# A decoder layer on one core: the recurrent gate stage and the compression MLP's first layer in a new order

## The chip, the cores and the metric

The kernel runs on one core of a Trainium2 chip. The metric is device time in microseconds (us). Before the change it is 1894.97 us, the median of three runs (1893.92 to 1895.76).

The engines are named as the profile names them: PE is TensorE (matmuls), DVE is VectorE, ACT is ScalarE, POOL is GpSimd, SP is SyncE, which issues most of the transfers.

## The reference, cut to what matters

One layer is computed for 512 tokens and 1024 features: a gated linear recurrence and a sparse attention side by side, then an expert layer, then a gated embedding. The change touches the recurrence (`rg_lru`, after a causal convolution of width 4) and the MLP that compresses keys and values.

```python
xa = causal_dwconv(z_rx, conv_w[i], conv_b[i])
ha = rg_lru(xa, lru_wr[i], lru_br[i], lru_wi[i], lru_bi[i], lru_lam[i])
...
def rg_lru(x, w_r, b_r, w_i, b_i, lam):
    xb = xf.reshape(B, S, RNN_BLOCKS, RNN_BLOCK)
    r = sigmoid(einsum('bsnc,ncd->bsnd', xb, w_r) + b_r)
    ig = sigmoid(einsum('bsnc,ncd->bsnd', xb, w_i) + b_i)
    log_a = -LRU_C * r * softplus(-lam)
    a = exp(log_a)
    u = sqrt(-expm1(2.0 * log_a)) * (ig * xf)
    # h[t] = a[t] * h[t-1] + u[t], along the 512 tokens
...
def compress_blocks(t, idx, pe, w1, b1, w2, b2):   # once for keys, once for values
    blk = t[:, idx] + pe[:, None, :]
    hid = gelu(einsum('bgnf,fh->bgnh', flat, w1) + b1)   # f = 32 * 128, h = 256
    return einsum('bgnh,hd->bgnd', hid, w2) + b2
```

## The kernel before, in words

Features lie on the 128 partitions and tokens along the free dimension. A projection of 1024 to 128 features is a *chunk*: 24 matmuls over 8 blocks k of the input. Every fp32 matrix is held as a rounded high half and a low half (the rest), and each product is three matmuls, high by high, high by low, low by high (`mm3`, L131 to L134; in the profile these three lines stand for nearly every matmul). The high half is a cast (`L126` on ACT, `L128` on DVE), the low half a subtraction (`L129`). Nothing reorders the work: each engine runs its instructions in the order in which the code is written, so the order of Python calls is the schedule.

The stages around the change, in the order in which PE runs them:

1. **Eight `rx` chunks (L398) and two `kc` chunks (L472).** After the matmuls of chunk c its evacuation `ev_rx` (L373) runs: ACT writes `xa` with the last convolution tap (L380), DVE adds the other three taps (L382), ACT and DVE make the two halves of `xa` (`xhl`), DVE and POOL the halves of the gate weights (`lwhl`). The two gate products (`lru`, six matmuls) of chunk c follow the matmuls of chunk c+1 on PE; then ACT takes two sigmoids (L394), and DVE multiplies the input gate by `xa` (L395, the *gate product*). Behind each chunk one piece of a list `side` is issued, small DVE and ACT work. Before each chunk, `look` splits the weights of the chunk two ahead: DVE casts, POOL subtracts (in this stage).
2. **Ten chunks `rg` and `vc` (L550 to L564)**, in the order rg 0 to 5, vc 0, vc 1, rg 6, rg 7 (all are called `z_rg` in the trace). Between the k blocks of a chunk stand the steps of `compress` (L479): the MLP's *first layer*, 16 steps for the keys and 16 for the values, four matmuls each (`hid`, L491). A step at block k of chunk n is called where the table `CSTEP[n]` holds k. Each step needs one piece of `w1` (128 x 512 fp32). POOL issues its load (L449) into one of four buffers, ACT casts its high half (L455), DVE subtracts its low half (L464), PE uses both; the low half frees the buffer for the piece four further on. `LAW` is 3: step n casts the high half of piece n+2 and makes the low half of piece n+1.
3. In the same chunks `SIDE[n]` deals out the recurrence, again by block k: `lru_b` (L403: tanh and two exponentials on ACT, one multiplication on DVE), two square roots of four blocks each (L415), `lru_c` (L418: one multiplication, L420, and one scan, L421, on DVE), and the rotary sine and cosine.
4. **Two `v` stages (L574)**: values of the selected and of the window branch. The last seven first-layer steps stand in the first. Then come the recurrent output `hg`, the `ks`, `kw` and `w_a` chunks, `q`, and the attention.

Of the 16 steps of the values three stand in rg 6 (its first entry in `CSTEP` is the transposition that ends the keys, `hidT`, L498), six in rg 7 and seven in the first `v` stage. They need `blk` (L436 and the two lines of its halves), which DVE makes from vc 0 and vc 1. Pieces are counted through both: the values' first step is 16.

Of the kernel before, what the change touches and what calls it, by code (L numbers as in the profile page):

```python
# [17 lines left out]
OP = mybir.AluOpType  # L18
# [76 lines left out]
def tile_hybrid(ctx, tc, a, out, dbg=None):  # L95
    nc = tc.nc
    V, A, T, G, SP = nc.vector, nc.scalar, nc.tensor, nc.gpsimd, nc.sync
# [17 lines left out]
    def bank(name, tag="ax"):  # L115
        if tag == "ax":
            tag = "aaax"[turn[0] % 4]
            turn[0] += 1
        return ps.tile([128, 512], F32, name=name, tag=tag, bufs=NBK[tag])

    def f(ap):
        return ap.bitcast(F32)

    def split(hi, lo, src, eng=None, heng=None):
        if heng is None:
            A.copy(hi, src)  # L126
        else:
            heng.tensor_copy(hi, src)  # L128
        (eng or V).tensor_tensor(lo, src, f(hi), op=OP.subtract)  # L129

    def mm3(o, sh, sl, mh, ml, start, stop):  # L131
        T.matmul(o, sh, mh, start=start, stop=False)  # L132
        T.matmul(o, sh, ml, start=False, stop=False)  # L133
        T.matmul(o, sl, mh, start=False, stop=stop)  # L134
# [45 lines left out]
    side = []  # L180

    def run_side(n):
        for _ in range(n):
            if side:
                side.pop(0)()

    def look(keys):
        for key in keys:
            if key not in ready:
                w8_split(key[0], key)  # L190
# [4 lines left out]
    def run_post():  # L195
        while post:
            post.pop(0)()

    def gemm(jobs, nside=1, nxt=()):

        keys = [j[:2] for j in jobs] + list(nxt)
        for n, (name, i, mh, ml, evac) in enumerate(jobs):
            look(keys[n:n + 3])
            w = ready.pop((name, i))
            o = bank("z_" + name)
            if key0 == keys[n]:
                for q, (ws, m) in enumerate(((0, mh), (1, mh), (0, ml))):
                    for k in range(KD):
                        T.matmul(o, w[:, ws, k], m[:, k], start=q == 0 and k == 0, stop=q == 2 and k == KD - 1)
            else:  # L210
                for k in range(KD):
                    mm3(o, w[:, 0, k], w[:, 1, k], mh[:, k], ml[:, k], k == 0, k == KD - 1)
            run_post()
            r = evac(i, o)
            if r is not None:
                post.append(r)
            run_side(nside[n] if isinstance(nside, tuple) else nside)
# [4 lines left out]
    nhi = keep.tile([128, KD, S], F32R, name="nhi", tag="nx")  # L222
    nlo = keep.tile([128, KD, S], F32R, name="nlo", tag="nx")
    rms = const.tile([128, 4, NT], F32, name="rms")

    def t2(nm, sh=(128, S), dt=F32):
        return p.tile(list(sh), dt, name=nm, tag="t2", bufs=4)
# [131 lines left out]
    gx = at.tile([128, 8, S], F32, name="gx", tag="big0")  # L359
# [6 lines left out]
    def load_lru(c):  # L366
        w = p.tile([128, 2, 128], F32, name="lruw", tag="lruw")
        SP.dma_start(w, a["lru_w"][c])
        lru_load.append(w)

    load_lru(0)

    def ev_rx(c, o):  # L373
        def col(b):
            return par[:, b + c:b + c + 1]

        def cw(j):
            return par[:, P_CW + c * 4 + j:P_CW + c * 4 + j + 1]
        xa = t2("xa")
        A.activation(xa, o, AF.Identity, bias=col(P_CB), scale=cw(3))  # L380
        for s in range(1, 4):
            V.scalar_tensor_tensor(xa[:, s:], o[:, :S - s], cw(3 - s), xa[:, s:], op0=OP.mult, op1=OP.add)  # L382
        w = lru_load.pop()
        if c < 7:
            load_lru(c + 1)
        xh, wh = xhl[:, c % 4], lwhl[:, c]
        split(wh[:, 0], wh[:, 1], w, G, V)
        split(xh[:, 0], xh[:, 1], xa)

        def gates():  # L390
            for j in range(2):
                o2 = bank("lru", "t")
                mm3(o2, wh[:, 0, j], wh[:, 1, j], xh[:, 0], xh[:, 1], True, True)
                A.activation(gx[:, c] if j else rr[:, c], o2, AF.Sigmoid, bias=col(P_BI if j else P_BR))  # L394
            V.tensor_tensor(gx[:, c], gx[:, c], xa, op=OP.mult)  # L395
        return gates

    gemm([("rx", i, nhi, nlo, ev_rx) for i in range(8)], nxt=[("kc", 0), ("kc", 1)])  # L398

    a2s = {}  # L400

# [27 lines left out]
    def ev_kv(j):  # L429
        def ev(c, o):  # L430
            if c == 0:
                blk[j] = at.tile([128, 2, 16, 2, NG, NB], F32R, name="blk", tag="sm2")
            for ab in range(2):
                pe = par[:, P_PE + 32 * j + 16 * ab:P_PE + 32 * j + 16 * ab + 16]
                t = t2("blkt", (128, 16, NB))
                V.tensor_tensor(t, o.rearrange("p (n l) -> p l n", l=16)[:, :, ab:ab + NB],  # L436
                                pe[:, :, None].to_broadcast([128, 16, NB]), op=OP.add)
                split(blk[j][:, ab, :, 0, c], blk[j][:, ab, :, 1, c], t, V, V)
        return ev
# [4 lines left out]
    w1n = [0, 0, 0]  # L444

    def w1_load(upto):
        while w1n[0] < min(upto, 32):
            j, l0 = divmod(w1n[0], 16)
            G.dma_start(w1buf[w1n[0] % 4], a["cmp_w1"][j][:, 2 * l0:2 * l0 + 2].rearrange("p l c -> p (l c)"))  # L449
            w1n[0] += 1  # L450
# [10 lines left out]
    def w1_lo(upto):  # L461
        while w1n[2] < upto:
            n = w1n[2]
            V.tensor_tensor(w1hl[:, n % 4, 1], w1buf[n % 4], f(w1hl[:, n % 4, 0]), op=OP.subtract)  # L464
            w1n[2] += 1
            w1_load(n + 5)
# [2 lines left out]
    V.tensor_tensor(sel, ident[:, 0:62], ident[:, 62:124], op=OP.add)  # L469
    w1_load(4)  # L470
    lo_eng[0] = V
    gemm([("kc", i, nhi, nlo, ev_kv(0)) for i in range(2)], nside=(2, 1), nxt=[("rg", 0), ("rg", 1)])  # L472

    kcT = at.tile([128, 2, NB], F32, name="kcT")
    vchi = at.tile([128, 2, 128], F32R, name="vchi")
# [69 lines left out]
    hls = [None, None]  # L545
    w1_split(1)
    seq = [("rg", i) for i in range(6)] + [("vc", 0), ("vc", 1)] + [("rg", i) for i in range(6, 8)]
    CSTEP = [(), (), (1, 3, 5, 7), (1, 3, 5, 7), (1, 3, 5, 7), (0, 2, 3, 5, 7), (), (), (4, 5, 6, 7), (0, 1, 3, 4, 6, 7)]
    SIDE = [(5,), (), (), (0, 0), (0, 0), (1,), (0, 0, 4), (0, 3, 6), (1, 2, 5), (1, 4, 6)]
    for n, key in enumerate(seq):  # L550
        look(seq[n:n + 3])
        w = ready.pop(key)
        o = bank("z_rg")
        for k in range(KD):
            mm3(o, w[:, 0, k], w[:, 1, k], nhi[:, k], nlo[:, k], k == 0, k == KD - 1)
            if k in CSTEP[n]:
                next(comp, None)
            run_side(SIDE[n].count(k))
            if n == 9 and k == 3:
                hls[0] = pair("vs")  # L560
                for j in range(2):
                    pair_split("vs", None, j, hls[0])
        (ev_rg if key[0] == "rg" else ev_kv(1))(key[1], o)
# [12 lines left out]
    for br, n in enumerate(("vs", "vw")):  # L576
        hl = hls[br]
        os = [bank("v") for _ in range(NT)]
        for i in range(NT):
            ts = slice(i * 128, (i + 1) * 128)  # L580
            for k in range(KD):
                T.matmul(os[i][:, :256], nhi[:, k, ts], hl[0][:, k], start=k == 0, stop=False)
                T.matmul(os[i][:, :256], nlo[:, k, ts], hl[0][:, k], start=False, stop=False)
                if br == 0 and k % 4 == 3:
                    next(comp, None)
        if br == 0:
            for _ in comp:
                pass
            hghi = at.tile([128, 8, S], F32R, name="hghi", tag="big0")
            hglo = at.tile([128, 8, S], F32R, name="hglo", tag="big1")  # L590
            hg += [hghi, hglo]
            side += [lru_d(c) for c in range(8)]
            split(wgh, wgl, wg)
            hls[1] = pair("vw")
            for j in range(2):
                pair_split("vw", None, j, hls[1])
        else:
            look([("ks", 0), ("ks", 1)])
        for i in range(NT):
            ts = slice(i * 128, (i + 1) * 128)  # L600
            for k in range(KD):
                T.matmul(os[i][:, :256], nhi[:, k, ts], hl[1][:, k], start=False, stop=k == KD - 1)
            split(vhi[:, i, br], vlo[:, i, br], os[i][:, :256])
            run_side(1)
    run_side(len(side))
    dump("kcT", kcT)
    dump("hg", f(hghi))
# [42 lines left out]
    def ev_q(c, o):  # L650
# [4 lines left out]
        def score():  # L655
# [9 lines left out]
         nxt=[("w_a", 0), ("w_a", 1)])  # L665
# [175 lines left out]
    for n in range(1, len(blocks) + 1):  # L841
# [5 lines left out]
        if n < len(blocks):  # L847
# [4 lines left out]
            i, hp = blocks[n]  # L852
# [38 lines left out]
    for q in range(4):  # L891
# [31 lines left out]
        for i in range(NT):  # L923
            if q < 3:
                wo_lo(i)
            if nhl and i == 0:
                for j in range(2):
                    c = slice(j * 128, (j + 1) * 128)
# [579 lines left out]
    for hf in range(2):  # L1508
        c = slice(hf * 512, (hf + 1) * 512)
# [82 lines left out]
```

## Time and profile before

| what | value |
|---|---|
| median of three runs | 1894.97 us |
| the profiled execution's own time | 1896.81 us |
| its span, first to last instruction | 1895.0 us |
| PE busy | 1819.3 us, 96% of the span |
| DVE busy | 1401.5 us, 74% |
| ACT busy | 840.3 us, 44% |
| POOL busy | 648.8 us, 34% |
| granted PE clock, mean of the run | 0.988 |
| the stages the change touches | from 30 us to some 190 us of the span |

The profile comes from one execution, whose own time is 1.84 us above the median of the timed runs; 1.81 us of its time lie outside the span. A busy share is an average: what an edit in one stage is worth is read from that stage's waits. In a timeline row the first number is the start in us from the span's start, the second the length; brackets at the end name idle time of the engine before the row and what ended it. Ends of matmuls are modelled, so the distance between the starts of two PE rows is a safer measure than their lengths.

### The profile page before, as it was taken

The numbers are of one execution on the slowest core, as the hardware profiler recorded it, in microseconds if no ns is written. First come the engines' busy times: TensorE is split into PE (matmuls) and PEld (weight loads), VectorE is DVE, ScalarE is ACT, GpSimd is POOL, SyncE is SP. The second block draws the span as 40 slices with busy tenths as digits, with TensorE's granted clock in tenths as the row PEclk, the third lists the DMA queues.
The fourth block names the chain that finished last, engine by engine and source line by source line (L and its number), as shares of the span: only waits on it lengthen the run. The fifth ranks groups of instructions, "written<-read, shape, count | busy, mean of one in ns | idle before, by whom it ended". The sixth has DMA issues, their size and how long they took to land.

```text
span 1895.0 us, 26509 instructions
## 1 busy us (share of the span) xinstructions
PE 1819.3 (96%) x9817; PEld 1594.3 (84%) x9817; DVE 1401.5 (74%) x2658; ACT 840.3 (44%) x1274; POOL 648.8 (34%) x419
## 2 busy tenths in 40 slices
PE   7998999999999989999999999999999999999997
PEld 6777888777789879899999888888888899999986
DVE  6867607565633378999999967888888788888864
ACT  4464333344522434574674763333333333333443
POOL 3311454322135325335335321222222255556400
PEclk9999999899999999999999999999999999999999
DMA  4353232211015426697787998999999899999941
GB/s 171 105 183 97 89 101 67 67 56 45 23 67 178 190 87 202 233 365 257 275 331 258 335 357 298 355 358 352 347 355 353 304 338 324 348 337 350 363 178 45
DMA packets 179810, 433.29 MB, mean 229 GB/s; under 512 B 14560, under 2 KB 88032, under 8 KB 179680
## 3 DMA queue, kind: packets, MB, share of 16 engines
q1 hardware_dynamic: 119664, 241.96, 36.8%
q0 software_dynamic: 40288, 145.77, 21.5%
q10 hardware_dynamic: 19728, 43.86, 6.1%
q8 instruction: 77, 1.26, 0.3%
q14 instruction: 53, 0.43, 0.1%
HBM read 382.25 MB, written 49.28 MB: 228 GB/s over the span
## 4 chain that ended last, share of the span: by engine, by line
PE 73%; DVE 16%; ACT 4%; issue 4%; DMA 3%; POOL 0%; SPq 0%; DVEq 0%; ACTq 0%; POOLq 0%
PE va L132 9%; PE va L134 9%; PE va L133 9%; PE xu L134 7%; PE xu L132 7%; PE xu L133 7%; DVE ul L1087 2%; DVE oh L1259 2%; DVE gr L1288 1%; PE G L1236 1%; PE z_m L132 1%; PE z_m L133 1%; PE z_m L134 1%; DVE acc L1294 1%; PE sc L996 1%
## 5 line engine op out<-in xcount | busy, mean ns | idle before, releaser
L132 PE MATMUL xu<-x2hi,uh 128*128 128x384 f32 x1008 | 345.2, 342 | 4.7 <-ACT ac L1097 4.7
L134 PE MATMUL xu<-x2hi,ul 128*128 128x384 f32 x1008 | 340.6, 338 | 5.8 <-DVE ul L1087 5.8
L133 PE MATMUL xu<-x2lo,uh 128*128 128x384 f32 x1008 | 339.9, 337 | 0.0
L132 PE MATMUL va<-v,A 128*128 128x512 f32 x768 | 299.0, 389 | 1.5 <-ACT A L126 1.5
L134 PE MATMUL va<-v,A 128*128 128x512 f32 x768 | 298.8, 389 | 0.0
L133 PE MATMUL va<-v,A 128*128 128x512 f32 x768 | 298.8, 389 | 0.0
L1273 POOL DMA_INDIRECT gr<-in_peer_u,eidx x128 | 170.7, 1333 | 327.8 <-DVE gr L1288 250.5
L1273 POOL DMA_INDIRECT gr<-in_peer_v,eidx x128 | 187.8, 1467 | 267.5 <-DVE acc L1294 210.2
L126 ACT CAST v<-vring 128x1024 fp32r<-128x1024 f32 x128 | 134.7, 1052 | 262.7 <-issue 144.2
L129 DVE TENSOR_TENSOR v<-vring,v 128x1024 fp32r<-128x1024 f32 x128 | 156.5, 1223 | 67.8 <-ACT v L126 67.2
L132 PEld LDWEIGHTS xu<-x2hi,uh 128*128 128x128 f32 x1008 | 191.4, 190 | 7.0 <-ACT ac L1097 5.3
L134 PEld LDWEIGHTS xu<-x2hi,ul 128*128 128x128 f32 x1008 | 191.1, 190 | 6.8 <-DVE ul L1087 6.8
L133 PEld LDWEIGHTS xu<-x2lo,uh 128*128 128x128 f32 x1008 | 191.4, 190 | 1.6
L134 PEld LDWEIGHTS va<-v,A 128*128 128x128 f32 x768 | 144.1, 188 | 30.4 <-DVE A L129 0.3
L132 PEld LDWEIGHTS va<-v,A 128*128 128x128 f32 x768 | 144.1, 188 | 29.9 <-ACT A L126 1.8
L133 PEld LDWEIGHTS va<-v,A 128*128 128x128 f32 x768 | 144.1, 188 | 28.3
L1294 DVE SCALAR_TENSOR_TENSOR acc<-gr,dots,acc 128x1024 f32<-128x1024 f32 x128 | 164.0, 1281 | 2.2 <-DMA gr<-in_peer_v,eidx 0.7
L1288 DVE SCALAR_TENSOR_TENSOR gr<-gr,x2g 128x1024 f32<-128x1024 f32 x128 | 158.1, 1255 | 8.3 <-DMA gr<-in_peer_u,eidx 8.2
L1082 ACT CAST uh<-ur 128x1024 fp32r<-128x1024 f32 x126 | 132.6, 1053 | 59.6 <-ACT ac L1097 29.2
L1097 ACT ACTIVATE ac<-xu 128x384 f32<-128x384 f32 x128 | 63.8, 499 | 195.4 <-PE xu L134 185.1
L1087 DVE TENSOR_TENSOR ul<-ur,uh 128x1024 fp32r<-128x1024 f32 x100 | 121.4, 1220 | 17.8 <-PE xu L134 8.3
L1239 ACT ACTIVATE gst<-G 128x512 f32<-128x512 f32 x96 | 100.4, 1160 | 13.9 <-PE G L1236 13.6
(450 smaller groups left out, 3617.0 us busy)
## 6 DMA issues: line engine op xcount, KB each, us to landing
vring<-in_peer_v SPq DMA_DIRECT2D x128, 512.0 KB
ur<-in_peer_uT SPq DMA_DIRECT2D x126, 512.0 KB
gdram<-gst ACTq DMA_DIRECT2D x12, 2048.0 KB
gt<-gdram SPq DMA_DIRECT2D x32, 768.0 KB
xdram<-ac ACTq DMA_DIRECT2D x88, 192.0 KB
vring<-xdram SPq DMA_DIRECT2D x88, 192.0 KB
raw_m<-in_w_in SPq DMA_DIRECT2D x16, 512.0 KB
raw_rx<-in_w_in SPq DMA_DIRECT2D x8, 512.0 KB
```

The source lines that it names most:

```text
L126: A.copy(hi, src)
L129: (eng or V).tensor_tensor(lo, src, f(hi), op=OP.subtract)
L132: T.matmul(o, sh, mh, start=start, stop=False)
L133: T.matmul(o, sh, ml, start=False, stop=False)
L134: T.matmul(o, sl, mh, start=False, stop=stop)
L1082: A.copy(us[e][0], urs[e])
L1087: (G if search[0] else V).tensor_tensor(us[e][1], urs.pop(e), f(us[e][0]), op=OP.subtract)
L1097: A.activation(ac, o[:, :ND], AF.Gelu_apprx_tanh)
L1239: A.activation(gst[:, :, c:c + 4].rearrange("p a t -> p t a"), o.rearrange("p (t a) -> p t a", t=4), AF.Copy, scale=1.0 / GSC)
L1273: G.indirect_dma_start(out=r, out_offset=None, in_=tab, in_offset=bass.IndirectOffsetOnAxis(ap=eidx[:, j:j + 1], axis=0))
L1288: V.scalar_tensor_tensor(r, r, 1.0, x2g, op0=OP.mult, op1=OP.mult, accum_out=dots[:, j:j + 1])
L1294: V.scalar_tensor_tensor(acc, r, dots[:, j:j + 1], acc, op0=OP.mult, op1=OP.add)
```

## The change

Four edits, all of order; no instruction is added or removed.

- The gate product of chunk c is no longer issued behind its two sigmoids; it is kept in a list `late` and issued in the evacuation of the next chunk, behind that chunk's convolution and halves. The last one goes to the front of `side` and is issued behind the evacuation of kc 0 (three pieces of `side` there, not two).
- At the end of a chunk (k = 7) whose successor has first-layer steps, the low half of every piece that is already cast is made at once (`w1_lo(w1n[1])`), ahead of the successor's weight split.
- `CSTEP`: rg 6 has steps at blocks 1, 6, 7 instead of 4, 5, 6, 7, and rg 7 seven steps instead of six.
- `SIDE`: the `lru_b` pieces go from block 0 to blocks 2 and 4 of their chunks; `lru_c` 1 moves from vc 1 to vc 0; of the other five, which stood in rg 6 and rg 7 (two and three), one stays in each, and three go into the first `v` stage (block 5 of its first three tiles). The pieces of `lru_d` come one per tile in the first `v` stage and two per tile in the second.

```diff
+    late = []
     def ev_rx(c, o):
...
-        split(wh[:, 0], wh[:, 1], w, G, V)
-        split(xh[:, 0], xh[:, 1], xa)
+        A.copy(xh[:, 0], xa)
+        V.tensor_copy(wh[:, 0], w)
+        V.tensor_tensor(xh[:, 1], xa, f(xh[:, 0]), op=OP.subtract)
+        G.tensor_tensor(wh[:, 1], w, f(wh[:, 0]), op=OP.subtract)
+        while late:
+            late.pop(0)()
...
-            V.tensor_tensor(gx[:, c], gx[:, c], xa, op=OP.mult)
+            late.append(lambda: V.tensor_tensor(gx[:, c], gx[:, c], xa, op=OP.mult))
...
+    side.insert(0, lambda: late.pop(0)())
...
-    CSTEP = [(), (), (1, 3, 5, 7), ..., (4, 5, 6, 7), (0, 1, 3, 4, 6, 7)]
+    CSTEP = [(), (), (1, 3, 5, 7), ..., (1, 6, 7), (0, 1, 2, 4, 5, 6, 7)]
...
+            if k == 7 and CSTEP[n + 1:n + 2] != [()]:
+                w1_lo(w1n[1])
...
+                if br == 0 and i < 3 and k == 5:
+                    run_side(1)
...
-            run_side(1)
+            run_side(1 + br)
```

What this does to the order on DVE in the `rx` stage: first the rows before, from the weight cast ahead of chunk 4 to that chunk's low half (`xa_414` belongs to chunk 3, `xa_474` to chunk 4).

```order
L128 CAST w8_435<-raw_rx_316 128x1024
L395 TENSOR_TENSOR gx_206<-gx_206,xa_414 128x512
L382 SCALAR_TENSOR_TENSOR xa_474<-z_rx_438,par_83,xa_474 128x511
L382 SCALAR_TENSOR_TENSOR xa_474<-z_rx_438,par_83,xa_474 128x510
L382 SCALAR_TENSOR_TENSOR xa_474<-z_rx_438,par_83,xa_474 128x509
L128 CAST lwhl_208<-lruw_419 128x256
L129 TENSOR_TENSOR xhl_207<-xa_474,xhl_207 128x512
```

And the same place now (`xa_413` belongs to chunk 3, `xa_473` to chunk 4):

```order
L128 CAST w8_435<-raw_rx_316 128x1024
L384 SCALAR_TENSOR_TENSOR xa_473<-z_rx_438,par_83,xa_473 128x511
L384 SCALAR_TENSOR_TENSOR xa_473<-z_rx_438,par_83,xa_473 128x510
L384 SCALAR_TENSOR_TENSOR xa_473<-z_rx_438,par_83,xa_473 128x509
L390 CAST lwhl_208<-lruw_418 128x256
L391 TENSOR_TENSOR xhl_207<-xa_473,xhl_207 128x512
L401 TENSOR_TENSOR gx_206<-gx_206,xa_413 128x512
```

The gate product has left the place between the cast of the weights and the convolution; it now stands behind the chunk's low half.

On ACT in the chunk rg 3, before (`a_922` and `a_927` are the recurrence steps of blocks 4 and 5; `w1half` and `w1buf` are pieces of the first layer's weights):

```order
L527 ACTIVATE gr<-z_rg 128x512
L406 ACTIVATE tt<-rr,pcoef 128x512
L407 ACT_TABLE_LOAD
L407 ACTIVATE a_922<-rr,n2coef 128x512
L408 ACTIVATE rr<-rr,ncoef 128x512
L406 ACTIVATE tt<-rr,pcoef 128x512
L407 ACTIVATE a_927<-rr,n2coef 128x512
L408 ACTIVATE rr<-rr,ncoef 128x512
L455 CAST w1hl<-w1half 128x512 x2
L455 CAST w1hl<-w1buf 128x512 x2
```

And now:

```order
L534 ACTIVATE gr<-z_rg 128x512
L462 CAST w1hl<-w1half 128x512
L413 ACTIVATE tt<-rr,pcoef 128x512
L414 ACT_TABLE_LOAD
L414 ACTIVATE a_935<-rr,n2coef 128x512
L415 ACTIVATE rr<-rr,ncoef 128x512
L462 CAST w1hl<-w1half 128x512
L413 ACTIVATE tt<-rr,pcoef 128x512
L414 ACTIVATE a_953<-rr,n2coef 128x512
L415 ACTIVATE rr<-rr,ncoef 128x512
L462 CAST w1hl<-w1buf 128x512 x2
```

The same eleven instructions; the first two casts stand ahead of the recurrence steps, one each.

On DVE where the values' first layer begins, before (from `blk` of vc 1 to the first low halves of `w1`):

```order
L436 TENSOR_TENSOR blkt<-z_rg,par 128x496
L128 CAST blk<-blkt 128x16x31
L129 TENSOR_TENSOR blk<-blkt,blk 128x16x31
L279 TENSOR_SCALAR sinT<-sinT,cst 128x512
L420 TENSOR_TENSOR gx<-gx,tt 128x512
L421 SCALAR_TENSOR_TENSOR rr<-rr,gx 128x512
L464 TENSOR_TENSOR w1hl<-w1buf,w1hl 128x512
L420 TENSOR_TENSOR gx<-gx,tt 128x512
L421 SCALAR_TENSOR_TENSOR rr<-rr,gx 128x512
L464 TENSOR_TENSOR w1hl<-w1half,w1hl 128x512 x2
```

And now (the first row is the low half of piece 17, the next one in `w1half` of piece 18, the last single one of piece 19):

```order
L471 TENSOR_TENSOR w1hl<-w1buf,w1hl 128x512
L443 TENSOR_TENSOR blkt<-z_rg,par 128x496
L128 CAST blk<-blkt 128x16x31
L129 TENSOR_TENSOR blk<-blkt,blk 128x16x31
L471 TENSOR_TENSOR w1hl<-w1half,w1hl 128x512
L279 TENSOR_SCALAR sinT<-sinT,cst 128x512
L427 TENSOR_TENSOR gx<-gx,tt 128x512
L428 SCALAR_TENSOR_TENSOR rr<-rr,gx 128x512
L471 TENSOR_TENSOR w1hl<-w1half,w1hl 128x512
L471 TENSOR_TENSOR w1hl<-w1buf,w1hl 128x512 x2
```

Piece 17's low half goes ahead of `blk`, piece 18's ahead of the sine and the scan; between the later pieces there is one scan where there were two.

## Rows read from the trace of the kernel before

**Rows 1.** The page's busy times: us, share of the span, instructions of each engine.

```profile
PE 1819.3 (96%) x9817; PEld 1594.3 (84%) x9817; DVE 1401.5 (74%) x2658; ACT 840.3 (44%) x1274; POOL 648.8 (34%) x419
```

**Rows 2.** PE's waits, 20 to 190 us: us in total, times, longest.

```profile
PE hid L491 <- DVE w1hl L464: 9.4, 9, 3.0
PE lru L132 <- ACT xhl L126: 2.0, 3, 1.2
PE lru L133 <- DVE xhl L129: 1.4, 4, 0.4
```

**Rows 3.** Timeline of PE, rx stage: start, length, operation, shape.

```profile
29.98 0.39 PE L132 MATMUL lru<-xhl,lwhl 128*128 128x512 f32 x1
...
38.59 0.39 PE L132 MATMUL z_rx<-nhi,w 128*128 128x512 f32 x1
...
44.04 0.39 PE L132 MATMUL lru<-xhl,lwhl 128*128 128x512 f32 x1
...
85.06 0.39 PE L132 MATMUL z_kc<-nhi,w 128*128 128x512 f32 x1
```

**Rows 4.** Timeline of DVE, POOL and ACT, rx stage.

```profile
40.18 2.32 DVE L382 SCALAR_TENSOR_TENSOR xa<-z_rx,par,xa 128x511 f32<-128x511 f32 x3
...
43.24 0.83 DVE L129 TENSOR_TENSOR xhl<-xa,xhl 128x512 fp32r<-128x512 f32 x1 [0.54 <-ACT xhl L126]
...
46.35 2.12 DVE L395 TENSOR_TENSOR gx<-gx,xa 128x512 f32<-128x512 f32 x1 [0.92 <-ACT gx L394]
...
39.73 2.78 POOL L129 TENSOR_TENSOR w<-raw_rx,w 128x1024 fp32r<-128x1024 f32 x1 [3.01 <-DVE w L128]
...
45.51 2.41 POOL L129 TENSOR_TENSOR w<-raw_rx,w 128x1024 fp32r<-128x1024 f32 x1 [1.99 <-DVE w L128]
...
46.21 0.77 ACT L380 ACTIVATE xa<-z_rx,par 128x512 f32<-128x512 f32 x1
```

**Rows 5.** Timeline of PE, first layer of the keys.

```profile
102.76 0.28 PE L491 MATMUL hid<-w1hl,blk 128*124 128x256 f32 x1
...
106.06 0.63 PE L491 MATMUL hid<-w1hl,blk 128*124 128x256 f32 x4
106.53 0.39 PE L132 MATMUL z_rg<-nhi,w 128*128 128x512 f32 x1
...
135.74 0.40 PE L132 MATMUL z_rg<-nhi,w 128*128 128x512 f32 x1
```

**Rows 6.** Timeline of ACT, chunk rg 3.

```profile
108.84 1.34 ACT L455 CAST w1hl<-w1buf 128x512 fp32r<-128x512 f32 x2 [5.10 <-DMA w1buf<-in_cmp_w]
110.08 0.59 ACT L527 ACTIVATE gr<-z_rg 128x512 f32<-128x512 f32 x1
...
113.97 0.70 ACT L406 ACTIVATE tt<-rr,pcoef 128x512 f32<-128x512 f32 x1
...
115.95 1.12 ACT L455 CAST w1hl<-w1half 128x512 fp32r<-128x512 f32 x2
...
118.19 0.62 ACT L455 CAST w1hl<-w1buf 128x512 fp32r<-128x512 f32 x1 [0.59 <-DMA w1buf<-in_cmp_w]
...
120.12 0.60 ACT L527 ACTIVATE gr<-z_rg 128x512 f32<-128x512 f32 x1
```

**Rows 7.** Timeline of DVE, chunk rg 6.

```profile
155.57 0.48 DVE L279 TENSOR_SCALAR sinT<-sinT,cst 128x512 f32<-128x512 f32 x1
...
157.83 0.67 DVE L464 TENSOR_TENSOR w1hl<-w1buf,w1hl 128x512 fp32r<-128x512 f32 x1
```

**Rows 8.** Timeline of PE, first layer of the values.

```profile
153.96 0.74 PE L491 MATMUL hid<-w1hl,blk 128*124 128x256 f32 x4 [1.23 <-DVE blk L129]
...
158.55 1.00 PE L491 MATMUL hid<-w1hl,blk 128*124 128x256 f32 x3 [3.04 <-DVE w1hl L464]
...
174.91 0.28 PE L582 MATMUL v<-w8vsh,nhi 128*128 128x256 f32 x1
```

**Rows 9.** Stretch by engine (PE, PEld, DVE, ACT, POOL), granted clock, DMA, GB/s.

```profile
158.00:163.00 5.00, 4.45 (x13) 3.58 (x14) 4.44 (x7) 1.21 (x2) 2.15 (x4) 0.51 0.27 72
```

More of the change, by code (lines that the diff above doesn't have):

```diff
@@ L471, in tile_hybrid @@
     lo_eng[0] = V
-    gemm([("kc", i, nhi, nlo, ev_kv(0)) for i in range(2)], nside=(2, 1), nxt=[("rg", 0), ("rg", 1)])
+    gemm([("kc", i, nhi, nlo, ev_kv(0)) for i in range(2)], nside=(3, 1), nxt=[("rg", 0), ("rg", 1)])
     kcT = at.tile([128, 2, NB], F32, name="kcT")
@@ L547, in tile_hybrid @@
     seq = [("rg", i) for i in range(6)] + [("vc", 0), ("vc", 1)] + [("rg", i) for i in range(6, 8)]
-    CSTEP = [(), (), (1, 3, 5, 7), (1, 3, 5, 7), (1, 3, 5, 7), (0, 2, 3, 5, 7), (), (), (4, 5, 6, 7), (0, 1, 3, 4, 6, 7)]
-    SIDE = [(5,), (), (), (0, 0), (0, 0), (1,), (0, 0, 4), (0, 3, 6), (1, 2, 5), (1, 4, 6)]
+    CSTEP = [(), (), (1, 3, 5, 7), (1, 3, 5, 7), (1, 3, 5, 7), (0, 2, 3, 5, 7), (), (), (1, 6, 7), (0, 1, 2, 4, 5, 6, 7)]
+    SIDE = [(5,), (), (), (2, 4), (2, 4), (2,), (0, 0, 3, 6), (3, 6), (7, 7), (5,)]
     for n, key in enumerate(seq):
```

## The prediction

> **What bounds the kernel now.** I read the page's busy times first, then PE's waits, then the timelines of PE, DVE and ACT where those waits lie. PE is busy 96% of the span [rows 1]: what PE stops waiting for comes off the end, unless it is given back. In the stages the change touches PE waits for three things: the low halves of the first layer's weights, 9.4 us in nine waits, and the two halves of `xa` ahead of the gate products, 2.0 and 1.4 us [rows 2]. That understates the loss, because a matmul behind a wait also starts with an empty pipeline. So I measure losses between marks: time between the starts of two PE rows, less the work between them at its pace where nothing waits.
>
> *The rx stage.* From the first gate pass (29.98) to the second kc chunk (85.06) are 55.1 us. In it lie seven chunks of 24 matmuls, 5.45 each (38.59 to 44.04), and eight gate passes of six matmuls, 1.36 each at that pace [rows 3]: 38.2 + 10.9 = 49.1. Lost: 6.0 us.
>
> *First layer of the keys.* From 102.76 to 135.74 are 33.0 us. In it lie 16 steps of 0.47 (106.06 to 106.53) [rows 5] and 84 chunk matmuls of 5.45 / 24 = 0.227: 7.5 + 19.1 = 26.6. Lost: 6.4 us.
>
> *First layer of the values.* From 135.74 [rows 5] to 174.91 [rows 8] are 39.2 us. In it lie 102 chunk matmuls (23.2), ten steps (4.7), and the transposition and the first eight half-width `v` matmuls, some 1.3 together: 29.2. Lost: 10.0 us. Single waits are 1.23 for `blk` and 3.04 for a low half [rows 8]; behind them the granted clock falls, 0.51 in the stretch 158 to 163, that is 1.2 GHz [rows 9].
>
> At most about 22 us can be won here. The count of instructions is the same on every engine; only waits can change.
>
> **The change part by part.**
>
> *Gate product behind the next convolution.* The trace shows why it hurts where it stands. At 46.35 it takes 2.12 us; POOL's weight subtraction began at 45.51 and took 2.41, so it ended at 47.92, and the product ended 0.55 later, about its length without POOL. The convolution, which reads PSUM and SBUF, ran its three taps in 2.32 while POOL worked from 39.73 on, undisturbed [rows 4]. So a product of two SBUF tiles waits for POOL, and the convolution, queued behind it on DVE, waits with it.
>
> The Trainium skill has this as a rule ("SBUF — State Buffer", section "SBUF: two separate sides"): VectorE with two SBUF inputs and GpSimd reading SBUF lock a port against each other for a whole instruction. The rule also speaks against the change, since the subtraction of the low half of `xa` reads two SBUF tiles too and stays on the path; what that would cost is the third rival.
>
> Without the product in front, the convolution starts when ACT has written `xa`: 46.21 + 0.77 = 46.98 instead of 48.47. From there to the end of the low half it takes as long as from 40.18 to 43.24 + 0.83 = 44.07 [rows 4], 3.9 us: 50.9. PE's next gate pass is due one pass and one chunk (6.8) after the one at 44.04 [rows 3]: 50.85, its first low half a matmul later. It fits, with nothing to spare. Two kinds of chunks still wait: chunk 1, whose `xa` is behind two table loads on ACT (0.4, as before), and those with long `side` work on DVE ahead of the weight cast: the ten small operations (0.1) and the four of the rotary angle (0.5). The product itself now falls between the low half and the side work; POOL's next subtraction starts only behind the weight cast that follows, so it meets nothing. Left over 1.2, with 0.2 for what the passes take above that pace. Gain 6.0 - 1.2 = **4.8**; bounds -4.5 (third rival) and 6.0.
>
> *Low halves ahead, keys.* The waits at the first steps of the chunks go: the half is made before the two-instruction weight split, not behind it. But ACT sets a pace here. From `gr` at 110.08 to the next at 120.12 are 10.04, of which it waited 0.59 for a transfer [rows 6]: 9.45 us of work for two recurrence steps, four casts, one `gr` and two table loads, in any order. PE needs 5.45 + 4 x 0.47 = 7.3 for the same chunk. ACT's run begins where it did, since the cast at the end of the pair at 108.84 waited for a transfer that is issued at the same time as before; so `gr` comes at 110.1, 119.5 and 129.0, whatever PE does. I follow the high halves from there: a cast 0.5, the recurrence step with its table load 3.4 (110.08 to 113.97, less `gr` at 0.5), another cast 0.5, the second recurrence step 2.0 (113.97 to 115.95) [rows 6].
>
> PE saves 1.4 at the first step and reaches rg 3 at 108.8. Steps 4 to 7 find their halves; rg 4 begins at 116.2. Step 8 waits 0.35 for its half (cast done 117.4, half 118.05). Step 11 is due at 123.5; its cast is the second behind the `gr` of 119.5, done 119.7 + 0.5 + 3.4 + 0.5 = 124.1, its half 0.67 later [length as in rows 7]: 1.2 of waiting. Step 12 is due at 125.9; its cast comes another 2.0 + 0.5 later, 126.6, its half 127.3: 1.3. Small ones 0.2. So 3.1 of the 6.4 stay. Gain **3.2**; bounds 0 (ACT's pace holds PE as much as now) and 6.4.
>
> *Steps dealt out anew, values.* Rg 5 ends about 3.1 earlier, and with it `gr`, the square roots and the first scan. DVE then needs the same work as before up to the first half of `blk`, which let PE go at 153.96, and one low half (0.67) more: 153.96 - 3.1 + 0.67 = 151.5. PE would be there at 150.1: 1.3 of waiting, as now. The next step, 3.04 today, finds its half done, since it is ahead of `blk`. Step 18 fits. Step 19 needs a half behind the second half of `blk`, the sine and one scan: sine and scan with their product took 157.83 - 155.57 = 2.3, and the second half of `blk` lay between 153.96 and 155.57, some 1.7 [rows 7, 8]. So the half of piece 19 is there at 151.4 + 1.7 + 0.6 + 2.3 + 0.6 = 156.6, the step due at 154.9: 1.5 with what it can start on. Two more waits of 0.7 follow, one behind the `vs` weight split and its casts, one behind the scan that stays in rg 7. With the three last scans in the `v` stage, where a step has 1.4 us instead of 1.15, the rest fits. Left over 4.3 of 10.0, and no stretch with PE idle as long as the 3.04. Gain **5.6**; bounds 2 (the clock falls again and every wait is half as long again) and 9.
>
> *The rest of the order.* `lru_d` two per tile is the same DVE work before the `ks` chunk; `w_a`, which needs it, is two stages away. The last gate product moves behind `blk` of kc 0; the second exponential buffer then waits some 0.3 for it on ACT, which has slack until rg 1 ends. I count zero for both; the cover is the `ks` and `kw` chunks, 4 x 5.45.
>
> **Sum.** 4.8 + 3.2 + 5.6 = 13.6 us. Everything later follows PE, so it starts earlier by that. The profiled execution takes 1896.81, which becomes 1883.2. The median of the runs is 1.84 lower, 1894.97, which becomes **1881.4**.
>
> **The rivals.**
>
> 1. *ACT's pace eats the keys, and the values gain less.* If ACT's 9.45 per chunk bounds PE as fully as now, the 3.2 are nothing; the values' gain stays, since their work does not hang on that pace, but starts no earlier relative to the square roots. 4.8 + 5.6 = 10.4: 1884.6. For it: ACT's two chunks leave no idle time [rows 6]. Against: the 6.4 lost were waits of PE that have ACT's pace in them only at the end.
>
> 2. *The clock falls again among the values.* Waits of 1.3 and 1.5 are less than 1.23 and 3.04, but of that kind. At 0.51 for five us 2.5 are lost [rows 9], and one wait more: gain 10: 1885.
>
> 3. *The lock changes its victim.* If each low half of `xa` meets POOL as the product at 46.35 did, it loses 2.12 - 0.6 = 1.5 in seven chunks, 10.5 us, where 6.0 are lost now. The first part is then -4.5 and the sum 4.3: 1890.7, at the edge of no change. Against: POOL's long subtraction starts behind the weight cast and is over before the low half is due; only its short one, on the gate weights, is near, and the halves at 43.24 already met that one (0.83).
>
> 4. *Slower: PE stays at 1.2 GHz.* If the waits of 1.3, 1.5, 0.7 and 0.7 keep the clock low from 151 to the end of the `v` steps, some 22 us of matmuls take twice as long: -22 against 13.6, 1903. It is slower by more than 0.2% from some 17 us of low clock on. Against: today the clock came back at 163 although waits of up to a microsecond followed.
>
> **How the numbers follow.** Forecast 0.62, rivals 0.14, 0.12, 0.07 and 0.05. A change under 0.2% (3.8 us) can't be told from none. Faster are the forecast and the first two, 0.88, less a little for what I have not thought of: 0.87. The third is split between same and faster; same 0.08, slower 0.05. The range takes in the first two rivals and the upper bounds in part (4.8 + 5.5 + 8): 1876.5 to 1889.
>
> **What would show it.** PE's waits for `xhl` fall from 3.4 to about 1; the gate product takes 0.7 in every chunk. PE's waits for `w1hl` from 9.4 to about 4, the largest at steps 11, 12 and 19, none of 3 us. No stretch at 0.5 of the clock between 150 and 175. The start of the `ks` chunk moves from 202 to about 188. Wrong would be: products still over 2 us; a low half of `xa` over 1 us; a PE wait over 2 us; or the same start earlier, but later stages giving it back.

## The result and the profile after

The changed kernel takes 1884.64 us (median of 13 runs) against 1895.03 for the kernel before beside it: ratio 0.9947, 95% interval 0.9935 to 0.9959, some 10 us faster. Forecast were 1881.4, with a range of 1876.5 to 1889. The profiled execution takes 1887.59 (span 1885.8, before 1895.0); it lies 2.95 above its median, where that of before lies 1.8 above, so the profiles show a gain of 9.2 and the medians one of 10.4. The lines below answer to those of before.

The page's busy times; the counts of [rows 1] stand, only waits have changed:

```profile
PE 1817.4 (96%) x9817; PEld 1594.2 (85%) x9817; DVE 1395.8 (74%) x2658; ACT 839.3 (45%) x1274; POOL 646.5 (34%) x419
```

PE's waits from 20 to 190 us (us in total, times, longest), against [rows 2]:

```profile
PE hid L498 <- DVE w1hl L471: 4.2, 7, 1.3
PE hid L498 <- DVE blk L129: 1.2, 1, 1.2
PE hid L498 <- ACT w1hl L462: 0.9, 2, 0.4
PE lru L133 <- DVE xhl L391: 0.6, 1, 0.6
```

The low halves still cost 4.2, where "about 4" was forecast, and the high halves at steps 11 and 12 another 0.9; of the rx stage one wait is left. PE's timeline of that stage, the marks of [rows 3]:

```profile
30.72 0.39 PE L132 MATMUL lru<-xhl,lwhl 128*128 128x512 f32 x1
...
80.35 0.50 PE L133 MATMUL lru<-xhl,lwhl 128*128 128x512 f32 x1 [0.58 <-DVE xhl L391]
...
81.61 0.39 PE L132 MATMUL z_kc<-nhi,w 128*128 128x512 f32 x1
```

50.9 us for 55.1. The gate product as a group (count, shortest, median and longest in ns), first of before, where three of the eight are long (2.12, 2.92 and 2.10 us), then of after:

```profile
L395 DVE TENSOR_TENSOR gx<-gx,xa x8: 684/712/2918, 32.7 to 86.0; 128x512 f32<-128x512 f32 x8
```

```profile
L401 DVE TENSOR_TENSOR gx<-gx,xa x8: 676/680/684, 37.9 to 86.4; 128x512 f32<-128x512 f32 x8
```

The keys' stage, 99.31 to 130.60, PE's timeline [rows 5]. From the row at 123.82 on the matmuls take longer; the one at 124.62 takes 0.63 instead of 0.39:

```profile
99.31 0.40 PE L498 MATMUL hid<-w1hl,blk 128*124 128x256 f32 x2
...
120.59 0.38 PE L498 MATMUL hid<-w1hl,blk 128*124 128x256 f32 x1 [0.41 <-ACT w1hl L462]
121.32 0.62 PE L498 MATMUL hid<-w1hl,blk 128*124 128x256 f32 x3 [0.35 <-DVE w1hl L471]
...
123.09 0.38 PE L498 MATMUL hid<-w1hl,blk 128*124 128x256 f32 x1 [0.45 <-ACT w1hl L462]
123.82 1.00 PE L498 MATMUL hid<-w1hl,blk 128*124 128x256 f32 x3 [0.34 <-DVE w1hl L471]
124.62 0.63 PE L132 MATMUL z_rg<-nhi,w 128*128 128x512 f32 x1
...
130.60 0.40 PE L132 MATMUL z_rg<-nhi,w 128*128 128x512 f32 x1
```

The same by stretch (columns as in [rows 9]): the granted clock is 0.62 right behind the two waits, part of the stretch at 1.2 GHz, and 1.00 where it was 0.51 before.

```profile
120.00:124.00 4.00, 2.45 (x10) 1.39 (x10) 1.62 (x3) 3.95 (x8) 0.54 (x1) 0.95 0.52 174
124.00:128.00 4.00, 4.00 (x15) 3.43 (x16) 3.97 (x6) 2.83 (x5) 2.10 (x3) 0.62 0.50 145
...
158.00:163.00 5.00, 3.96 (x23) 3.02 (x22) 4.97 (x7) 1.81 (x3) 1.11 (x3) 1.00 0.82 278
```

The values and what follows, PE's timeline: the waits forecast (1.3 for `blk`, 1.5 at step 19), and one of those in the `v` tiles that were not (step 27, at 168.65). `ks` starts at 193.37, where about 188 was forecast:

```profile
149.43 0.73 PE L498 MATMUL hid<-w1hl,blk 128*124 128x256 f32 x4 [1.15 <-DVE blk L129]
...
154.62 0.62 PE L498 MATMUL hid<-w1hl,blk 128*124 128x256 f32 x3 [1.33 <-DVE w1hl L471]
...
164.59 0.28 PE L591 MATMUL v<-w8vsh,nhi 128*128 128x256 f32 x1
...
168.65 0.62 PE L498 MATMUL hid<-w1hl,blk 128*124 128x256 f32 x3 [0.78 <-DVE w1hl L471]
...
193.37 0.40 PE L132 MATMUL z_ks<-nhi,w 128*128 128x512 f32 x1
```

What step 27 waits for, on ACT and then on DVE: its high half is cast by 166.43, but its low half, at 167.93, stands on DVE behind one of the scans moved into `v` and the scan's multiplication (at 166.07):

```profile
165.82 0.61 ACT L462 CAST w1hl<-w1half 128x512 fp32r<-128x512 f32 x1
```

```profile
166.79 1.22 DVE L428 TENSOR_TENSOR_SCAN rr<-rr,gx 128x512 f32<-128x512 f32 x1
167.93 0.67 DVE L471 TENSOR_TENSOR w1hl<-w1half,w1hl 128x512 fp32r<-128x512 f32 x1
```

### The profile page after: what moved, and what is told of

It reads as the page before. It is cut to its first block, busy times and chain, and to the rows that moved or that the text cites. A ratio compares the mean times of both kernels' runs of the same rounds, so it can differ in the third digit from the quotient of the medians.

```text
span 1885.8 us, 26512 instructions
## 1 busy us (share of the span) xinstructions
PE 1817.4 (96%) x9817; PEld 1594.2 (85%) x9817; DVE 1395.8 (74%) x2658; ACT 839.3 (45%) x1274; POOL 646.5 (34%) x419
## 4 chain that ended last, share of the span: by engine, by line
PE 74%; DVE 14%; issue 4%; ACT 4%; DMA 3%; SPq 0%; POOL 0%; DVEq 0%; ACTq 0%; POOLq 0%
PE va L132 9%; PE va L133 9%; PE va L134 9%; PE xu L134 7%; PE xu L132 7%; PE xu L133 7%; DVE ul L1098 2%; DVE oh L1270 2%; DVE gr L1299 1%; PE G L1247 1%; PE z_m L132 1%; PE z_m L133 1%; PE z_m L134 1%; DVE acc L1305 1%; PE z_w_a L134 1%
## 5 line engine op out<-in xcount | busy, mean ns | idle before, releaser
L129 DVE TENSOR_TENSOR v<-vring,v 128x1024 fp32r<-128x1024 f32 x128 | 156.5, 1222 | 66.9 <-ACT v L126 66.7
L1250 ACT ACTIVATE gst<-G 128x512 f32<-128x512 f32 x96 | 100.3, 1159 | 13.6 <-PE G L1247 13.3
```

Of the source, the lines that this page charges most:

```text
L1250: A.activation(gst[:, :, c:c + 4].rearrange("p a t -> p t a"), o.rearrange("p (t a) -> p t a", t=4), AF.Copy, scale=1.0 / GSC)
```

## The experiments

All times of stages are differences between the marks of the prediction, in one profile each: rx from the first gate pass to the second kc chunk, keys to behind the last step, values to the `v` matmuls behind step 25, v from there to the first `ks` matmul. The 17.7 us between rx and keys are the same in every kernel. The column "to ks" is their sum with these 17.7, first gate pass to `ks`; a ratio compares with runs of the kernel before made beside that kernel's. The gate pass itself starts between 29.98 and 31.41 in kernels whose code before it is the same, so starts are compared after taking this off.

| kernel | rx | keys | values | v | to ks | median us | ratio (95%) |
|---|---|---|---|---|---|---|---|
| before | 55.1 | 33.0 | 39.2 | 26.9 | 171.9 | 1895.0 | |
| after | 50.9 | 31.3 | 34.0 | 28.8 | 162.7 | 1884.6 | 0.9947 (0.9935 to 0.9959) |
| 1 gate part alone | 50.9 | 33.4 | 39.5 | 26.9 | 168.4 | 1891.1 | 0.9975 (0.9963 to 0.9986) |
| 2 keys part alone | 52.9 | 29.8 | 39.6 | 27.2 | 167.2 | 1892.7 | 0.9990 (0.9978 to 1.0002) |
| 3 values part alone | 55.2 | 33.8 | 34.0 | 28.3 | 169.1 | 1892.6 | 0.9985 (0.9977 to 0.9994) |
| 4 gate read from PSUM | 50.3 | 33.5 | 39.3 | 26.9 | 167.8 | 1888.1 | 0.9963 (0.9953 to 0.9974) |
| 5 after, gelu deferred | 50.9 | 27.5 | 34.0 | 28.8 | 159.0 | 1881.6 | 0.9926 (0.9913 to 0.9940) |
| 6 after, roots earlier | 50.9 | 32.0 | 35.1 | 28.0 | 163.6 | 1887.4 | 0.9951 (0.9934 to 0.9967) |
| 7 both | 50.9 | 27.7 | 33.6 | 29.2 | 159.1 | 1881.6 | 0.9924 (0.9911 to 0.9936) |
| 8 both, gate from PSUM | 50.3 | 27.5 | 33.6 | 29.6 | 158.7 | 1880.4 | 0.9925 (0.9910 to 0.9940) |
| 9 8, vs split apart | 50.3 | 27.2 | 29.4 | 35.2 | 159.8 | 1883.9 | 0.9928 (0.9913 to 0.9943) |
| 10 9, tail mended | 50.4 | 27.0 | 29.4 | 29.0 | 153.4 | 1877.3 | 0.9912 (0.9895 to 0.9929) |
| 11 9, vw low on DVE | 50.4 | 27.0 | 29.4 | 32.1 | 156.5 | 1877.7 | 0.9911 (0.9896 to 0.9926) |

Runs of one kernel lie some 4 to 12 us apart, so the columns of stages tell more than the medians; the interval of number 2 takes in 1, so its time alone does not tell it from before. What follows `ks`, nearly the same code in every kernel, takes between 1687.5 and 1693.9 us in these profiles. One profile stands for each row, and stages with the code of before differ too: rx from 52.9 to 55.2, the keys from 33.0 to 33.8.

**1 to 3: each part alone.** Number 1 is the kernel before with the diff's lines on `late`; 2 and 3 share out the rest:

```diff
 2  SIDE of rg 3 to 5 as in the change, and behind run_side:
+            if k == 7 and 1 <= n <= 4:
+                w1_lo(w1n[1])
 3  CSTEP, SIDE from chunk 6 on, run_side in v as in the change, and:
+            if k == 7 and n >= 7:
+                w1_lo(w1n[1])
```

> The kernel before with the first part alone: gate products queued behind the next convolution. Theory (each part wins in its own stage): from the first gate pass to the second kc chunk 55.1 us become 50.9, as in the changed kernel; the product takes 0.7 in every chunk; the keys' stage (rg 2 to 5) stays at 33.0 and the values' (to the second tile of v) at 39.2. Time some 4 us less, 1891. Rival (the waits only move on): the keys' stage, which then begins 4 us earlier against its transfers and against ACT, loses 2 to 4 us of it, and the time is within 2 us of before.

> The kernel before with low halves one chunk ahead for the keys alone (and the recurrence steps of rg 3 to 5 at their new places); gate product, values and v steps as before. Theory: the waits at the first step of a chunk go, those at steps 11 and 12 (0.8 each, from ACT's pace) come, the keys' stage takes 31 to 31.6 instead of 33.0, with or without a short stretch at half clock behind step 12; 1.5 to 2 us less in all. Rival (the gain of this stage in the changed kernel came from the earlier end of rx, not from the low halves): 33.0 stays.

> The kernel before with the third part alone: steps and scans of the values dealt out anew, low halves ahead in the last chunks; rx and keys as before. Theory: the 3.0 us wait becomes about 1.3, the stretch at half clock between 158 and 163 goes, the values' stage takes 34 instead of 39.2, and the first v tiles give 1 to 2 back: start of ks some 3.5 us earlier than 201.8. Rival (the scans moved into v cost there all that they free): start of ks within 1 us of 201.8.

Each part wins in its own stage: 4.2 in rx, 3.2 among the keys, 5.1 among the values, of which v gives 1.4 back. No rival holds, though `ks` comes 2.8 earlier by the marks in number 3 and not 3.5: its keys, with the code of before, took 0.8 more. Two surprises lie in number 2. Its keys take 29.8 and not 31.3: the waits at steps 11 and 12 are there as in the changed kernel, but the clock doesn't fall behind them. These are the stretches that lie about the two waits as 120 to 124 and 124 to 128 do in the changed kernel; PE is busy for the same 2.45 us in the first:

```profile
121.86:125.86 4.00, 2.45 (x10) 1.39 (x10) 1.62 (x3) 3.95 (x8) 0.54 (x1) 1.00 0.47 161
125.86:129.86 4.00, 4.00 (x23) 3.46 (x24) 3.97 (x6) 2.79 (x5) 2.09 (x3) 1.00 0.50 153
```

And its rx, with the code of before, is 2.2 shorter than there: the product of the fourth chunk took 2.92 us in the one (at 54.48) and 0.69 in the other, so that two of the eight are long here and not three (DVE's timeline, number 2):

```profile
55.15 0.69 DVE L395 TENSOR_TENSOR gx<-gx,xa 128x512 f32<-128x512 f32 x1
```

So the loss in rx is itself a matter of whether two instructions meet.

**4: the port or the place?** Nothing is moved; the product's operand changes its memory:

```diff
-                A.activation(gx[:, c] if j else rr[:, c], o2, AF.Sigmoid, ...)
-            V.tensor_tensor(gx[:, c], gx[:, c], xa, op=OP.mult)
+                A.activation(o2 if j else rr[:, c], o2, AF.Sigmoid, ...)
+            V.tensor_tensor(gx[:, c], o2, xa, op=OP.mult)
```

> The kernel before with nothing moved: ACT writes the second gate (sigmoid) back into its PSUM bank and the product reads that bank instead of an SBUF tile. Theory (a product of two SBUF tiles waits for POOL's instruction): the product takes 0.7 to 0.8 in every chunk with POOL at work beside it, though it stands where it stood, and rx's 55.1 fall to 51 to 52. Rival (the product is late or slow for its place in DVE's queue, or POOL and DVE share SBUF bandwidth in every instruction): it stays at 2 us in most chunks and rx at 54 to 55.

All eight products take 0.69, and the one at 47.05 does so with POOL's subtraction under way (the product as a group, then POOL's and DVE's timelines):

```profile
L395 DVE TENSOR_TENSOR gx<-lru,xa x8: 680/690/692, 33.4 to 81.9; 128x512 f32<-128x512 f32 x8
```

```profile
46.22 2.40 POOL L129 TENSOR_TENSOR w<-raw_rx,w 128x1024 fp32r<-128x1024 f32 x1 [1.98 <-DVE w L128]
```

```profile
47.05 0.69 DVE L395 TENSOR_TENSOR gx<-lru,xa 128x512 f32<-128x512 f32 x1 [0.92 <-ACT lru L394]
```

In [rows 4] the same pair gave 2.12. The rival's "most chunks" misread the kernel before, where three of eight were long. The place was no cost: rx falls by 4.7, more than moving the product wins (4.2).

**5: one gelu later.**

```diff
+        if n == 3:
+            o3 = o
+            continue
         (ev_rg if key[0] == "rg" else ev_kv(1))(key[1], o)
+        if n == 4:
+            ev_rg(3, o3)
```

> The changed kernel with one instruction moved: the gelu of rg 3 runs behind that of rg 4, so ACT loads one pair of tables less (2.56 us) ahead of steps 11 and 12. Theory (ACT's order makes those two waits, and the waits the half-clock stretch behind them): no PE wait for a first-layer half over 0.3 us between 116 and 126, clock 1.00 from 120 to 132, the keys' stage 27 to 28 instead of 31.3; start of ks some 3.5 us earlier than 193.4. Rival 1 (the halves come late for their transfers, not for ACT): waits of the same length remain, now on a transfer. Rival 2 (the half clock comes by itself): the waits go and the stretch stays; the keys' stage 29.5.

ACT's timeline shows the cast going straight into the recurrence step, without a table load, and the two gelus under one load:

```profile
114.61 0.61 ACT L462 CAST w1hl<-w1half 128x512 fp32r<-128x512 f32 x1
115.12 0.72 ACT L413 ACTIVATE tt<-rr,pcoef 128x512 f32<-128x512 f32 x1
...
120.77 1.28 ACT L534 ACT_TABLE_LOAD   x1
122.06 1.09 ACT L534 ACTIVATE gr<-z_rg 128x512 f32<-128x512 f32 x2
```

The two waits are gone, and with them the half clock: PE is busy throughout, at 1.00.

```profile
120.00:124.00 4.00, 4.00 (x24) 3.47 (x24) 3.43 (x5) 3.97 (x7) 2.09 (x3) 1.00 0.78 248
124.00:128.00 4.00, 4.00 (x24) 3.43 (x23) 2.28 (x4) 1.79 (x4) 1.61 (x3) 1.00 0.92 297
```

The keys take 27.5, 3.8 less; neither rival holds.

**6 to 8: the roots earlier.**

```diff
-    side += [sqrt, sqrt] + [c0 to c2] + [rot_c, rot_d] + [c3 to c7]
+    side += [sqrt, sqrt, rot_c] + [c0 to c2] + [rot_d] + [c3 to c7]
-    SIDE = [(5,), (), (), (2, 4), (2, 4), (2,), (0, 0, 3, 6), (3, 6), (7, 7), (5,)]
+    SIDE = [(5,), (), (), (2, 4), (2, 4), (2, 5, 5, 5), (0, 0, 3, 3), (3,), (), ()]
-                if br == 0 and i < 3 and k == 5:
+                if br == 0 and (i, k) in ((0, 0), (2, 5), (3, 0), (3, 5)):
```

(The last line stands ahead of the step here.) Number 7 adds 5, number 8 the edit of 4 in place of `late`.

> The changed kernel with the two square roots and the sine moved ahead of the gelu of rg 5 on ACT, so that three scans and the sine's product lie on DVE ahead of the values' blocks, no scan between the blocks and step 24, and the last three scans behind step 29 of the first v tiles. Theory (DVE's queue is what makes the waits at step 19 and in the v tiles): the 1.33 wait at step 19 and those of 0.34 and 0.78 among the v tiles go, blk's 1.15 stays; values 34.0 becomes 31.5 to 32.5, v 28.8 becomes 27; start of ks some 3.5 us earlier. Rival (the casts on ACT and their transfers pace these steps): waits move from DVE to ACT or a transfer, and ks starts within 1 us of 193.4.

> Both of these in the changed kernel. Theory: the gains add, ks starts 6.5 to 7.5 us earlier than 193.4 and the time is some 6 us under the changed kernel's. Rival (with the keys earlier, ACT or the transfers become the values' pace): no more than 4.

> As the last, but with the gate product where the kernel before has it and its gate read from PSUM, not moved behind the next convolution. Theory (the port, not the place, cost the 6 us): rx takes 50.3 as in the run with nothing but that edit, 0.5 less than with the moved product; else as the last: some 0.5 us less. Rival: moving wins more than the PSUM operand once the rest of DVE's queue is tighter; 1 to 2 us more.

The theory of 6 fell in its number: `ks` comes 1.0 later by the marks, not 3.5 earlier. The wait at step 19 went, as it said, but one of 2.26 came at step 22. Of the waits in the `v` tiles the one at step 26 (0.34) went in 6, but stands again, and longer, in 7 and 8 (0.7 and 1.1); the one at step 27 stayed (0.77), and in all three a scan, now that of block 4, still stands on DVE ahead of its low half. Moving the scans out of the way there was not tested by 6. In number 7 (DVE, then ACT) the low halves of two pieces stand behind the split of the `vs` weights, for whose casts DVE waits 3.19 us with nothing to do; the loads behind these halves leave late, and four steps on a cast waits for one of them:

```profile
149.24 1.28 DVE L471 TENSOR_TENSOR w1hl<-w1buf,w1hl 128x512 fp32r<-128x512 f32 x2
153.71 2.36 DVE L129 TENSOR_TENSOR w8vsl<-raw_vs,w8vsh 128x1024 fp32r<-128x1024 f32 x2 [3.19 <-ACT w8vsh L126]
155.98 1.28 DVE L471 TENSOR_TENSOR w1hl<-w1half,w1hl 128x512 fp32r<-128x512 f32 x2
```

```profile
152.62 1.99 ACT L126 CAST w8vsh<-raw_vs 128x1024 fp32r<-128x1024 f32 x2
...
161.74 0.62 ACT L462 CAST w1hl<-w1half 128x512 fp32r<-128x512 f32 x1 [5.57 <-DMA w1half<-in_cmp_w]
```

So 7 stays where 5 is (its rival: "no more than 4"), and 8 wins 0.6 in rx, as its theory said.

**9 to 11: the vs split, and the tail.**

```diff
 9  (on 8)
-            if n == 9 and k == 3:        # both halves of vs: cast, subtract
+            if n == 9 and k in (3, 6):   # one cast each; subtractions in vlow
+                if br == 0 and (i, k) == (0, 0):
+                    while vlow: vlow.pop(0)()
+                    ring.prefetch(ring.used + 3)   # the loads of the next weights
   c3 behind step 20; c4 to c7 at (2, 5), (3, 0), (3, 3), (3, 5)
 11 (on 9)  vw: lo_eng V instead of G
 10 (on 11) only the products of c4 to c7 there, their scans in v's second half,
     with two pieces of side per tile in both v stages
```

> The last kernel with the weight split of vs taken apart: its two casts on ACT three products apart, its two subtractions on DVE only behind step 24 (the first half of v needs the high part alone); and the scan that stood ahead of the values' second block is put behind step 20, the others behind step 29. Theory (what holds the values now is DVE standing in the vs split for ACT, 3.2 us, with two finished casts' low halves queued behind it, and the scan ahead of blk): the 2.24 wait at step 22 falls under 0.6, the 1.40 for blk goes, and as the loads behind those halves start 2 us earlier, the waits in the v tiles (0.79, 0.34, 0.76) shrink to under 1 in all; values 33.6 becomes 30 to 31, ks starts 3.5 us earlier than 189.7, the time is some 3 us less. Rival (the transfers of the first layer, four buffers deep, pace the steps): the waits turn into waits for ACT's casts that wait for a transfer; values 32.5 or more, ks under 1.5 us earlier.

> The last kernel with its tail mended in two ways: the last four scans run in the second half of v, only their products stay in the first; and the low half of the vw weights is subtracted on DVE instead of POOL. Theory (the first half of the edit before gained 4.2 us among the values; v gave it back because the four scans stood ahead of what v's second half needs, two of their instructions stretched from 1.23 and 0.69 to 3.28 and 2.76 beside POOL's 5.84): the 4.67 wait in v goes, with it the half clock behind it; v takes 27 to 28 instead of 35.2, ks starts near 183, the time is 6 to 7 us under the changed kernel plus deferral (1881.6), some 1875. Rival (the evacuation of v is late for another reason, a bank or ACT): v stays above 32 and ks after 188.

> The kernel before the last (vs split taken apart) with only the vw low halves moved from POOL to DVE, the four scans left where they are, ahead of v's second half. Theory (POOL's subtraction locks DVE's two-SBUF instructions): the four products and scans take 0.69 and 1.23 each with nothing stretched, 4.1 us of the stretching goes; DVE now does the subtraction itself (2.4), so the 4.67 wait falls to 2 to 3 and v from 35.2 to 32 or 33. Rival (the stretched scans are slow for another reason than POOL): they stay at 3.3 and 2.8.

Number 9 does among the values what it said: 29.4, where the prediction counted 29.2 of work, with no wait for `blk` or a half over 0.3. But v takes 5.6 us more, and `ks` comes 1.0 later by the marks instead of 3.5 earlier. DVE and POOL there:

```profile
168.87 3.28 DVE L421 TENSOR_TENSOR_SCAN rr<-rr,gx 128x512 f32<-128x512 f32 x1
172.07 2.76 DVE L420 TENSOR_TENSOR gx<-gx,tt 128x512 f32<-128x512 f32 x1
```

```profile
168.44 2.63 POOL L129 TENSOR_TENSOR w8vwl<-raw_vw,w8vwh 128x1024 fp32r<-128x1024 f32 x1 [9.52 <-ACT w8vwh L126]
```

The scan and the product that meet POOL's two subtractions (the second follows on the first) last 2 us longer each, v's evacuation waits behind them, and PE waits 4.67 and then runs at half clock (PE's timeline and the stretch after it):

```profile
176.73 0.58 PE L596 MATMUL v<-w8vwh,nhi 128*128 128x256 f32 x1 [4.67 <-DVE vv L129]
```

```profile
176.00:180.00 4.00, 3.27 (x15) 3.27 (x16) 2.85 (x10) 1.47 (x5) 0.00 (x0) 0.50 0.27 110
```

Number 11 takes the subtractions off POOL and leaves the rest. The same instructions have their usual lengths, and the wait of 4.67 becomes one of 2.79, within the 2 to 3 forecast:

```profile
167.66 1.23 DVE L421 TENSOR_TENSOR_SCAN rr<-rr,gx 128x512 f32<-128x512 f32 x1
168.80 0.67 DVE L420 TENSOR_TENSOR gx<-gx,tt 128x512 f32<-128x512 f32 x1
169.50 1.23 DVE L421 TENSOR_TENSOR_SCAN rr<-rr,gx 128x512 f32<-128x512 f32 x1
```

With the scans put later as well, number 10 loses the last long wait; its v takes 29.0 where 27 to 28 were forecast, its time is 1877.3 where some 1875 were. PE's waits, 20 to 190 us:

```profile
PE v L601 <- DVE vv L129: 0.4, 1, 0.4
PE hid L493 <- DVE w1hl L466: 0.3, 1, 0.3
PE lru L133 <- DVE xhl L129: 0.3, 1, 0.3
PE hid L493 <- ACT w1hl L457: 0.3, 1, 0.3
```

It beats both kernels: 1877.3, some 7 us under the changed one (the intervals against before, 0.9895 to 0.9929 and 0.9935 to 0.9959, don't meet). Against 11 it gains 3.1 us up to `ks`, which the medians (1877.3 and 1877.7) don't tell apart.

## Why the prediction came out as it did

*Gate product: 4.8 forecast, 4.2 measured, alone or with the rest.* The cause was named rightly: the product waits for POOL when both its operands are in SBUF. Experiment 4 shows it by the operand, 11 by the other engine. The Trainium skill's rule ("SBUF — State Buffer", section "SBUF: two separate sides"), an exclusive lock for a whole instruction, agrees with both: the meetings read here cost 1.4 to 2.2 us each. The 6.0 lost before is that of the one profile that the forecast read; with two meetings instead of three the same code lost 3.8 in number 2. The third rival (the lock moves to the low half of `xa`) came in small only; the eight of them as a group (shortest, median and longest in ns), and the last:

```profile
L391 DVE TENSOR_TENSOR xhl<-xa,xhl x8: 824/854/1039, 29.4 to 79.3; 128x512 fp32r<-128x512 f32 x8
```

```profile
79.25 1.04 DVE L391 TENSOR_TENSOR xhl<-xa,xhl 128x512 fp32r<-128x512 f32 x1 [0.33 <-ACT xhl L389]
```

That is the 0.83 of [rows 4], at worst 0.2 more. The 0.6 that is missing is in the "left over", 1.2 forecast and 1.8 measured (50.9 less the 49.1 of work). Three chunks behind long `side` work on DVE hold it. There the low half takes 1.00, 1.03 and 1.04; it starts 0.25 to 0.3 behind the start of POOL's short subtraction of the gate weights (79.00 for the one shown), which takes 0.74. PE loses 0.20, 0.25 and 0.87 there by the starts of its gate passes, 1.3 in all, where 0.1 and 0.5 were counted for this work. The step that failed is the argument against the third rival that such a meeting costs nothing, since the half at 43.24 took 0.83 in one; that half started 0.46 behind POOL's.

*Keys: 3.2 forecast, 1.7 measured.* The waits came at steps 11 and 12 as worked out, and ACT's pace was 9.35 for the 9.45 assumed; the idle times shown there are 0.8 a step, but by the starts of PE's rows each step loses 1.2 (number 2, without the clock), where 1.2 and 1.3 were forecast. What failed is the step "3.1 of the 6.4 stay": no clock was counted in it. The matmuls from 123.8 to 127.1 ran at half speed, which cost the missing 1.5. Alone (2) this part gave the 3.2; with the waits removed (5) it gave 5.4 and the clock stayed up. The prediction had the falling clock as its second rival, but looked for it among the values alone.

*Values: 5.6 forecast, 5.2 measured,* with the waits for `blk` and at step 19 within 0.2 of the forecast, and no half clock there.

*"With the three last scans in the v stage ... the rest fits": it did not.* v takes 1.9 longer, and by the starts of PE's rows steps 26, 27 and 29 hold all of it (0.6, 1.05 and 0.2). At step 27 the scan is the cause, as the rows of DVE and ACT above show. Step 26 waits for a cast; in numbers 7 and 8 this cast waits for its load, which leaves late behind two low halves that stand on DVE behind the `vs` split. In the changed kernel the load leaves behind the same two halves (160.16), though the profile names PE for the cast's wait. Number 9 puts the scans behind step 29 and takes the `vs` split apart, and both waits are gone; each cause is read from the rows, and no kernel takes away one alone.

*Sum.* 4.2 + 1.7 + 5.2 - 1.9 = 9.2 of 13.6 up to `ks`; the profiled executions differ by the same 9.2. (By its own terms the forecast left 3.3 among the keys and 5.7 among the values, not 3.2 and 5.6; 0.2 in all.) The time fell 3.2 us above the forecast and inside the range. That it is the 1884.6 of the first rival, and near the 1885 of the second, is chance, since neither was the mechanism: ACT's pace did not eat the keys' gain, and the clock fell in another stage. Whether it falls there is chance too, as far as these runs show; number 2 had the same waits without it. The fourth did not come: each fall of the clock lasted a few us.

## What to carry to other kernels

Where DVE reads two SBUF tiles beside a long POOL instruction, look at that instruction's longest time, not its mean; putting one operand in PSUM, or the other engine's work elsewhere, cures it without a new order. When a cast, its low half and its next load form a ring, find what stands on DVE ahead of the low half of a finished cast: here a scan of 1.2 us with its product, or a split for which DVE itself stood waiting. That, not the amount of work, set the pace here. Count the clock with every pair of waits over a microsecond that you forecast, in each stage.

## What the runs showed of the hardware that was not expected

- Granted clock: two waits of 0.8 within 4 us, in which PE was busy for 2.45, were followed by 0.62 in the changed kernel and by 0.60 in number 6, while the same waits with the same 2.45 left 1.00 in number 2. Waits of 2.26 (number 6) were followed by 0.77 over four us, those of 2.23 (number 7) by 1.00. Neither the length of a wait nor PE's work in the four us about it decides; what does is open.
- Scans meet the lock as products do: 1.23 became 3.28 beside POOL's subtraction.
- A table load is 1.28 on ACT with the next instruction right behind it (120.77 + 1.28 = 122.05, the gelu starts at 122.06). The Trainium skill ("ScalarE: Activation LUTs", section "What ACT_TABLE_LOAD costs") gives about 2.66 us with a drain; no such drain stands in these rows.
